# One load of decays for each head, behind the fetch of the triangular blocks, and a later rank for their work on ScalarE

## The chip, the cores and the metric

The kernel runs on one core of a Trainium2 chip. The metric is the device time of one execution in microseconds (us). The kernel before takes 782.92 us, the median of three runs (780.73, 782.92 and 783.98). A profile of one execution stands beside the runs; its own time is given with it below.

The engines are called PE (TensorE, matrix products), DVE (VectorE), ACT (ScalarE), POOL (GpSimd) and SP (SyncE, which here only issues transfers).

## What is computed

One layer of a decoder for 16 meta tokens and 512 tokens of width 1024, all in float32. Softmax attention and a chunked gated DeltaNet, 8 heads each, run side by side on the same normalised input; their gated outputs are merged, projected and normalised. The change lies in the DeltaNet branch, which for one head of 128 channels and chunks of tokens computes this (shortened from the reference):

```python
gc = jnp.cumsum(g, axis=-1)                      # log decays, summed within a chunk
diff = gc[..., :, None] - gc[..., None, :]
decay = jnp.where(incl, jnp.exp(diff), 0.0)      # incl: lower triangle with its diagonal
m = jnp.where(strict, einsum('bhnid,bhnjd->bhnij', kb, k) * decay, 0.0)
t_inv = triangular_solve(m + eye, eye, left_side=True, lower=True, unit_diagonal=True)
a_intra = einsum('bhnid,bhnjd->bhnij', q, k) * decay
q_dec = q * jnp.exp(gc)[..., None]
...
v_new = u_c - w_c @ state                        # chunk after chunk
o_c = qd_c @ state + a_c @ v_new
state = state * cd_c + kd_c.T @ v_new
```

So a head's summed log decays gc are used twice: in the matrix of decays (diff and decay) and in exp(gc), by which q is multiplied.

## The kernel before

**Planner.** The kernel is written as some dozens of generators (tasks). A task yields the name of an engine before it emits instructions on it, the name of an event that it waits for, or a tuple with the name of a buffer that it wants. A planner in the same file (class Plan, lines 82 to 192) runs all tasks against its own estimates of durations and so fixes the order of the instructions on every engine when the program is built. Among the tasks that want an engine it takes the one that can begin first, and among equals the one of lower rank; `spawn(gen, rank)` (line 107) sets the rank, and without one a task inherits the rank of the task that spawned it. On the chip each engine works its instructions off in that order; an instruction waits only for the data and the buffers that it needs, not for the planner's events. A load is reckoned by `transfer` (lines 127 to 131): it arrives 600 + 460 ns after its issue, plus its bytes at 360 bytes a nanosecond, plus 20 and 900 ns, later if other loads are under way.

**Tasks and ranks.** `dense` (rank 4) issues the big products of the projections, one block of 128 output channels after another: for each pair of heads k, v and q of the DeltaNet, then the attention's k, q, gate and v, and so on. A weight block is loaded (tile raw, four buffers), split by a cast on ACT (wh) and a subtraction on DVE (wl) into a high and a low part, and used in three passes; two blocks fit in split form. What follows a product (copies from the accumulator on ACT into xp or vT, the convolution and its tanh and gate: `conv_silu`, line 760) has rank 1. The pairs of heads of the DeltaNet (`delta_pair`, line 901) have rank 0, the attention heads rank 2.

**A pair of heads, gi.** `delta_pair` spawns for each of its two heads `decay`, `keys`, `values` and `products` (lines 1140 to 1144):

- `decay` (line 916) takes one of two buffers E, loads the head's row of summed log decays from a scratch tensor in DRAM (gcd) to all 128 partitions (256 KB), and makes the matrix of decays in place: four ACT instructions (Relu with a bias), one ACT exponential, one mask on POOL. For the second and later pairs it starts as soon as a buffer E is given back.
- `keys` and `values` transpose k and v on PE and evacuate them on ACT with scales (tiles ktd and vr).
- `products` (line 1007) multiplies k by k and k by q on PE. DVE evacuates the products with E into MT (the matrix m) and AT (a_intra). Four small DMAs per head write MT's diagonal 32 x 32 blocks to a scratch tensor (scrm), and E is given back (line 1069). Then the task takes the one buffer eg, loads the same row of gcd a second time, takes its exponential on ACT and multiplies q by it on DVE (lines 1070 to 1078).

When all blocks of a pair are written, they are fetched into the tile msub by two DMAs (`fetch`, line 1160), with two groups of blocks on separate partitions. Then DVE inverts them by forward substitution: 31 steps (line 1167) of two instructions each (tmps, then ts). The result goes through DRAM again (scrt, then td), and PE assembles the inverses of the chunks; `steps` (line 1319) runs the recurrence. Meanwhile the attention takes its turns with its scores (accumulator psc, ACT exponentials e, DVE maxima ast).

The buffers are counted in the dictionary SLOTS (line 68). `kernel` (line 1939) builds the program; it reserves 4096 bytes of scratch on each partition for DMAs whose descriptors software writes.

Of the kernel before, what the change touches and what calls it, by code (L numbers as in the profile page):

```python
# [10 lines left out]
F32 = mybir.dt.float32  # L11
F32R = mybir.dt.float32r
BF16 = mybir.dt.bfloat16
AF = mybir.ActivationFunctionType
ALU = mybir.AluOpType
# [3 lines left out]
P = 128  # L19
# [6 lines left out]
NC = SEQ // P  # L26
# [7 lines left out]
def dense_order():  # L34
# [11 lines left out]
    for p in range(KB // 2):  # L46
# [17 lines left out]
PE, DVE, ACT, POOL, SP = "PE", "DVE", "ACT", "POOL", "SP"  # L64

SLOTS = dict(raw=4, w=2, wo=4, W=4, sn=5, st=1, tf=1, psc=1, xp=2, y=2, kT=2, qT=2, ktd=2, vr=2, E=2, eg=1, AT=2, MT=2, sc=2, km=1,
             ts=1, msub=1, TT=1, aq=2, ak=1, vT=1, vs=1, e=4, pT=2, pm=2, ao=1, th=8)


# [10 lines left out]
class Plan:  # L82
# [24 lines left out]
    def spawn(self, gen, rank=None):  # L107
        time, src = self.here() if self.task else (0.0, SP)
        self.tasks.append(Task(gen, self.task.rank if rank is None else rank, time, src))

    def done(self, event):
        self.events[event] = self.here()
# [142 lines left out]
def hybrid_block(ctx: ExitStack, tc: tile.TileContext, x, meta, wblk, wbd, wout, pcol, prow, out):  # L255
    nc = tc.nc
    plan = Plan({**SLOTS, "wo": 0}, BANKS, ALL_BANKS)
    T, V, A, G, S = (Engine(plan, n, e) for n, e in
                     ((PE, nc.tensor), (DVE, nc.vector), (ACT, nc.scalar), (POOL, nc.gpsimd), (SP, nc.sync)))
    spawn, done = plan.spawn, plan.done  # L260
# [9 lines left out]
    def mk(pl, shape, dt, tag, bufs=None):  # L270
        uid[0] += 1
        kw = {} if bufs is None else {"bufs": bufs}
        return pl.tile(shape, dt, tag=tag, name=f"{tag}_{uid[0]}", **kw)
# [6 lines left out]
    dp = dctx.enter_context(tc.tile_pool(name="dp", bufs=1))  # L280
# [5 lines left out]
    def bank(kind):  # L286

        return mk(ps, [P, 2, 512], F32, kind, SLOTS[kind]) if kind == "psc" else banks_[plan.task.slot]

    def give(kind, at=None):  # L290
        plan.give(kind, names_.index(at.tensor.name) if kind in BANKS else 0)

    def slot(pl, shape, dt, tag):
        return mk(pl, shape, dt, tag, SLOTS[tag])

# [5 lines left out]
    def tick(event, n):  # L301
        ticks[event] = ticks.get(event, 0) + 1
        if ticks[event] == n:
            done(event)
# [3 lines left out]
    mt = mk(sp, [P, 2 * P], F32, "mt")  # L308
# [18 lines left out]
    msub = mk(dp, [P, 32, 32], F32, "msub")  # L327
# [59 lines left out]
    def split(n, raw):  # L387

        yield ("w" if n < len(ORDER) or n - len(ORDER) in (4, 5) else "wo",)
        if n < len(ORDER) or n - len(ORDER) in (4, 5):  # L390
            wh, wl = (mk(wp, [P, D], F32R, t, SLOTS["w"]) for t in ("wh", "wl"))
        else:
# [166 lines left out]
    def gates():  # L559
# [179 lines left out]
        late["ap"] = actx.enter_context(tc.tile_pool(name="ap", bufs=1, side="right"))  # L739
        late["pm"] = [mk(late["ap"], [P, 3, 32], F32R, f"pm{n}") for n in range(SLOTS["pm"])]  # L740
        late["vm"] = mk(late["ap"], [96, P], F32R, "vm")
# [11 lines left out]
    def chunk(c, o=NM):  # L753
        return slice(o + P * c, o + P * (c + 1))

    xps = [mk(dp, [P, L + 3], F32, f"xp{n}") for n in range(SLOTS["xp"])]
    for t in xps:
# [143 lines left out]
    def delta_pair(gi):  # L901
        hs = (2 * gi, 2 * gi + 1)
        E_, name = {}, lambda t: f"{t}/{gi}"
        kd, vr, at, mt = {}, {}, {}, {}
        scr = tc.dram_tile([33, 32, 32], F32, name=f"scrm{gi}")
        scrt = tc.dram_tile([33, 32, 32], F32, name=f"scrt{gi}")
        yield "ap"
# [1 line left out]
        sc = slot(dp, [P, 2, 4, 8], F32, "sc")  # L909
        yield ("km",)  # L910
        km, vm = slot(dp, [P, 32], F32, "km"), mk(dp, [P, 32], F32, "vm", SLOTS["km"])

        def gc_row(h):
            return gcd.rearrange("(c h) t -> h c t", h=8)[h].unsqueeze(0).broadcast_to([P, NC, P])

        def decay(i):

            h = hs[i]
            yield ("E",)
            e = slot(dp, [P, NC, P], F32, "E")  # L920
            yield SP
            S.dma_start(out=e, in_=gc_row(h))
            for c in range(NC):
                yield ACT
                A.activation(out=e[:, c, :], in_=e[:, c, :], func=AF.Relu, bias=gc[:, c, h:h + 1], scale=-1.0)
            yield ACT
            A.activation(out=e, in_=e, func=AF.Exp, scale=-1.0)
            yield POOL
            G.affine_select(out=e, in_=e, pattern=[[0, NC], [1, P]], base=0, channel_multiplier=-1,
                            compare_op=ALU.is_ge, fill=0.0)  # L930
            E_[i] = e
            done(f"E{h}")
# [74 lines left out]
        def products(i):  # L1007
            h = hs[i]
            yield f"dq{h}"
            yield f"dk{h}"  # L1010
            k = pair["k", h]
            q = pair["q", h]

            def norms():
                yield ("pdl",)
                yield PE
                pt = bank("pdl").rearrange("p (c d) -> p c d", d=P)
                for c in range(NC):
                    T.transpose(pt[:, c, :], q[:, chunk(c, 0)], ident)
                for c in range(NC):  # L1020
                    yield ACT
                    A.activation(out=mk(dp, [P, P], F32, "sqk", 1), in_=pt[:, c, :], func=AF.Square,
                                 accum_out=sc[:, i, c, qe_:qe_ + 1])
                give("pdl", pt)
                yield DVE
                V.tensor_scalar(out=sc[:, i, :, qe_], in0=sc[:, i, :, qe_], scalar1=128 * EPS, scalar2=128 * EPS * 4e-6,
                                op0=ALU.mult, op1=ALU.add)
                done(f"qe{h}")

            yield f"E{h}"  # L1030
            yield f"s{h}"
            yield ("MT",)
            mt[i] = slot(dp, [P, NC, P], F32, "MT")
            yield ("AT",)
            at[i] = slot(dp, [P, NC, P], F32, "AT")
            for c2 in range(0, NC, 2):
                yield ("pdl",)
                yield PE
                pg = bank("pdl").rearrange("p (c x) -> p c x", x=2 * P)
                for c in (c2, c2 + 1):  # L1040
                    T.matmul(pg[:, c - c2, 0:P], k[:, chunk(c)], k[:, chunk(c)], start=True, stop=True)
                    T.matmul(pg[:, c - c2, P:2 * P], k[:, chunk(c)], q[:, chunk(c, 0)], start=True, stop=True)

                def evac(c2=c2, pg=pg):
                    for c in (c2, c2 + 1):
                        yield DVE
                        V.scalar_tensor_tensor(out=mt[i][:, c, :], in0=pg[:, c - c2, 0:P], scalar=sc[:, i, c, s_:s_ + 1],
                                               in1=E_[i][:, c, :], op0=ALU.mult, op1=ALU.mult)
                    tick(f"m{h}", 2)
                    yield DVE  # L1050
                    V.tensor_tensor(out=at[i][:, c2:c2 + 2, :], in0=pg[:, :, P:2 * P], in1=E_[i][:, c2:c2 + 2, :], op=ALU.mult)
                    give("pdl", pg)
                    tick(f"a{h}", 2)

                spawn(evac())
            spawn(norms())
            yield f"m{h}"
            for b in range(4):

                def put(b=b):  # L1060
                    yield SP
                    S.dma_start(
                        out=scr[16 * i:16 * i + 16].rearrange("(c b) j i -> b j c i", b=4)[b],
                        in_=mt[i][32 * b:32 * b + 32, :, 32 * b:32 * b + 32])
                    tick(name("scr"), 9)

                spawn(put())
            yield f"a{h}"
            give("E")
            yield ("eg",)  # L1070
            yield SP
            eg = slot(dp, [P, NC, P], F32, "eg")
            S.dma_start(out=eg, in_=gc_row(h))
            yield ACT
            A.activation(out=eg, in_=eg, func=AF.Exp)
            yield DVE
            V.tensor_tensor(out=q, in0=q, in1=eg.rearrange("p c t -> p (c t)"), op=ALU.mult)
            give("eg")
            done(f"qd{h}")

# [57 lines left out]
            tick(name("scr"), 9)  # L1138

        for i in range(2):  # L1140
            spawn(decay(i))
            spawn(keys(i))
            spawn(values(i))
            spawn(products(i))
# [22 lines left out]
        for j in range(31):  # L1167
            n, w = 31 - j, min(j + 1, 16)
# [3 lines left out]
                            in1=ts_[0:97, j, 0:w].unsqueeze(1).broadcast_to([97, n, w]), op=ALU.mult)  # L1172
# [723 lines left out]
    def deltas():  # L1896
        for gi in range(H // 2):
            spawn(delta_pair(gi))
            yield "ap"
# [54 lines left out]
```

## Time and profile before

| | before |
|---|---|
| median of 3 runs | 782.92 us |
| profiled execution, whole time | 781.9 us |
| its span, first to last instruction | 780.1 us |
| granted TensorE clock, mean | 0.996 |
| PE busy | 752.8 us (96%) |
| DVE busy | 566.0 us (73%) |
| ACT busy | 477.2 us (61%) |
| POOL busy | 68.3 us (9%) |
| issues of E from gcd, and of eg from gcd | 8 and 8, 256 KB each |

In rows of the timeline the columns are the start in us, the busy time in us, the engine, the line, the operation, output and inputs, their shapes, the count; a bracket gives the engine's idle time just before and who ended it. All operations have line 220, a helper that records each of them, so rows are told apart by their tiles: `MT<-bank,sc,E` writes MT from an accumulator bank, sc and E. A q behind an engine's name (SPq) marks its queue: such a row is the issue of a transfer, not its landing. In rows of stretches the columns are the stretch, its length, the busy time and count of PE, of its weight loads, of DVE, ACT and POOL, then the granted clock of PE as a share of full speed, the DMA engines' share and GB/s. Heads are counted from 0, pairs too: pair 1 is heads 2 and 3.

### The profile page before, as it was taken

The page shows a single profiled execution, that of the slowest core. Times are in us where ns is not written, and L with a number is a line of the kernel's source. Part 1 is how long each engine was busy: PE and PEld are TensorE (multiplying, and loading weights), DVE is VectorE, ACT ScalarE, POOL GpSimd, SP SyncE. Part 2 cuts the span into 40 slices and gives each one's busy share as a digit, 9 for nine tenths or more (in the row PEclk, how much of TensorE's full clock was granted, in tenths as well). Part 3 has the DMA queues.
Part 4 walks back from the last instruction along what each step waited for, and adds up shares of the span by engine and source line. Part 5 has one row for each costly group of instructions (what it writes and reads, how often), then busy time and mean ns, then how long its engine had stood idle before and what let it go on. Part 6 is the DMA issues. An engine that isn't in the chain of part 4 may idle for free.

```text
span 780.1 us, 14404 instructions
## 1 busy us (share of the span) xinstructions
PE 752.8 (96%) x5479; PEld 689.1 (88%) x5479; DVE 566.0 (73%) x1287; ACT 477.2 (61%) x1272; POOL 68.3 (9%) x98
## 2 busy tenths in 40 slices
PE   5999999999999999999999999999999999999996
PEld 4999788999987899998789998888988998899786
DVE  6767698477769767767956766995678868789553
ACT  5375747688564768765486975467776436444432
POOL 3120002021000202100020220000000000000001
PEclk9999999999999999999999999999999999999999
DMA  8132533111333301234220124222023322332702
GB/s 307 32 116 70 120 102 72 52 55 56 112 99 89 88 29 55 68 111 115 82 68 29 56 80 124 88 82 69 28 66 100 134 58 105 108 109 85 266 0 109
DMA packets 45470, 70.10 MB, mean 90 GB/s; under 512 B 20273, under 2 KB 28881, under 8 KB 45401
## 3 DMA queue, kind: packets, MB, share of 16 engines
q1 hardware_dynamic: 45400, 69.18, 28.8%
q8 instruction: 43, 0.70, 0.4%
q14 instruction: 27, 0.21, 0.1%
HBM read 65.98 MB, written 3.19 MB: 89 GB/s over the span
## 4 chain that ended last, share of the span: by engine, by line
PE 70%; DVE 11%; DMA 9%; ACT 5%; issue 2%; SPq 2%; POOL 1%; POOLq 0%; ACTq 0%; DVEq 0%
PE bank L220 66%; PE psc L220 3%; DMA msub<-scrm 3%; DVE wl L220 2%; DMA eg<-gcd 2%; DVE tmps L220 2%; SPq L220 2%; DVE ts L220 2%; DMA scrt<-ts 2%; ACT wh L220 1%; DMA td<-scrt 1%; DMA xt<-in_x_dram 1%; DVE aq L220 1%; ACT E L220 1%; DMA E<-gcd 1%
## 5 line engine op out<-in xcount | busy, mean ns | idle before, releaser
L220 PE MATMUL bank<-hnH,wh 128*128 128x512 f32 (+3 forms) x944 | 317.4, 338 | 1.0 <-ACT hnH L220 0.8
L220 PE MATMUL bank<-hnH,wl 128*128 128x512 f32 (+3 forms) x944 | 302.3, 322 | 2.3 <-DVE wl L220 2.3
L220 PE MATMUL bank<-hnL,wh 128*128 128x512 f32 (+3 forms) x944 | 301.9, 322 | 0.0
L220 PEld LDWEIGHTS bank<-hnH,wl 128*128 128x128 f32 x944 | 177.6, 189 | 17.2 <-DVE wl L220 3.2
L220 PEld LDWEIGHTS bank<-hnH,wh 128*128 128x128 f32 x944 | 178.0, 189 | 14.6 <-ACT hnH L220 1.0
L220 PEld LDWEIGHTS bank<-hnL,wh 128*128 128x128 f32 x944 | 178.1, 190 | 10.2
L220 DVE TENSOR_TENSOR wl<-raw,wh 128x1024 fp32r<-128x1024 f32 x82 | 100.3, 1223 | 51.9 <-ACT wh L220 51.0
L220 ACT CAST wh<-raw 128x1024 fp32r<-128x1024 f32 x82 | 86.0, 1048 | 39.5 <-PE bank L220 24.1
L220 DVE SCALAR_TENSOR_TENSOR y<-xp,pc,y 128x528 f32<-128x528 f32 (+1 forms) x72 | 54.2, 756 | 1.4 <-ACT y L220 0.4
L220 ACT ACTIVATE e<-psc,ast 128x144 f32<-128x144 f32 (+3 forms) x64 | 34.4, 539 | 23.1 <-DVE ast L220 18.6
L220 DVE TENSOR_TENSOR tmps<-msub,ts 97x240 f32<-97x240 f32 (+27 forms) x124 | 39.1, 316 | 7.6 <-DMA msub<-scrm 5.7
L220 DVE TENSOR_TENSOR ts<-ts,tmps 97x240 f32<-97x240 f32 (+27 forms) x124 | 39.7, 320 | 2.2
L220 PE MATMUL bank<-btH,Wh 128*128 128x256 f32 x128 | 35.9, 280 | 0.0
L220 PE MATMUL bank<-btL,Wh 128*128 128x256 f32 x128 | 35.7, 279 | 0.0
L220 PE MATMUL bank<-btH,Wl 128*128 128x256 f32 x128 | 35.7, 279 | 0.0
L220 PE MATMUL psc<-ak,aq 128*128 128x264 f32 (+3 forms) x160 | 29.4, 305 | 4.1 <-ACT e L220 4.1
L220 ACT CAST Wh<-raw 128x1024 fp32r<-128x1024 f32 (+1 forms) x24 | 21.7, 906 | 17.7 <-PE bank L220 11.6
L220 PEld LDWEIGHTS psc<-ak,aq 128*128 128x128 f32 x160 | 23.7, 189 | 6.7 <-ACT e L220 5.4
L220 DVE TENSOR_TENSOR Wl<-raw,Wh 128x1024 fp32r<-128x1024 f32 (+1 forms) x24 | 24.9, 1044 | 6.4 <-ACT Wh L220 6.3
L220 DVE TENSOR_REDUCE ast<-psc 128x1 f32<-128x528 f32 (+3 forms) x40 | 28.5, 714 | 0.2
L220 ACT ACTIVATE sqk<-bank 128x128 f32<-128x128 f32 x64 | 17.8, 278 | 13.5 <-PE bank L220 12.5
L220 ACT COPY sn<-bank 128x256 f32<-128x256 f32 x24 | 9.0, 374 | 26.5 <-PE bank L220 26.4
(335 smaller groups left out, 1508.8 us busy)
## 6 DMA issues: line engine op xcount, KB each, us to landing
raw<-in_wblk_dram SPq DMA_DIRECT2D x96, 512.0 KB, 3.5
raw<-in_wout_dram SPq DMA_DIRECT2D x8, 512.0 KB, 5.2
xt<-in_x_dram SPq DMA_DIRECT2D x4, 512.0 KB, 3.5
E<-gcd SPq DMA_DIRECT2D x8, 256.0 KB, 6.0
eg<-gcd SPq DMA_DIRECT2D x8, 256.0 KB, 6.0
xr<-in_x_dram SPq DMA_DIRECT2D x8, 256.0 KB
out_dram<-xr SPq DMA_DIRECT2D x8, 256.0 KB, 2.1
msub<-scrm SPq DMA_DIRECT2D x8, 132.0 KB
```

Source lines behind the costliest of these rows:

```text
L220: return real(*args, **kw)
```

## The change

- `decay` has a second output: after the load of E it takes a buffer eg, writes the exponential of E into it on ACT, and goes on with E as before. `products` uses this eg and no longer loads or computes it. There are two buffers eg in place of one, and they are held from `decay` to the multiplication of q.
- For all pairs but the first, `decay` waits in the planner for the event that the previous pair's triangular blocks have been fetched (msub).
- `decay` is spawned with rank 2 in place of the inherited 0. This covers its load, its ACT instructions and its mask.
- The scratch for DMAs by software is 1024 bytes in place of 4096.

```diff
-... E=2, eg=1, ...
+... E=2, eg=2, ...
...
-        kd, vr, at, mt = {}, {}, {}, {}
+        kd, vr, at, mt, eg = {}, {}, {}, {}, {}
...
         def decay(i):

             h = hs[i]
+            if gi:
+                yield f"msub/{gi - 1}"
             yield ("E",)
             e = slot(dp, [P, NC, P], F32, "E")
             yield SP
             S.dma_start(out=e, in_=gc_row(h))
+            yield ("eg",)
+            eg[i] = slot(dp, [P, NC, P], F32, "eg")
+            yield ACT
+            A.activation(out=eg[i], in_=e, func=AF.Exp)
             for c in range(NC):
                 yield ACT
                 A.activation(out=e[:, c, :], in_=e[:, c, :], func=AF.Relu, bias=gc[:, c, h:h + 1], scale=-1.0)
...
             yield f"a{h}"
             give("E")
-            yield ("eg",)
-            yield SP
-            eg = slot(dp, [P, NC, P], F32, "eg")
-            S.dma_start(out=eg, in_=gc_row(h))
-            yield ACT
-            A.activation(out=eg, in_=eg, func=AF.Exp)
             yield DVE
-            V.tensor_tensor(out=q, in0=q, in1=eg.rearrange("p c t -> p (c t)"), op=ALU.mult)
+            V.tensor_tensor(out=q, in0=q, in1=eg[i].rearrange("p c t -> p (c t)"), op=ALU.mult)
             give("eg")
...
         for i in range(2):
-            spawn(decay(i))
+            spawn(decay(i), 2)
             spawn(keys(i))
...
-    nc = _bacc.Bacc("TRN2", target_bir_lowering=False, num_devices=1, dynamic_dma_scratch_size=4096)
+    nc = _bacc.Bacc("TRN2", target_bir_lowering=False, num_devices=1, dynamic_dma_scratch_size=1024)
```

More of the change, by code (lines that the diff above doesn't have):

```diff
@@ L64 @@
 PE, DVE, ACT, POOL, SP = "PE", "DVE", "ACT", "POOL", "SP"
-SLOTS = dict(raw=4, w=2, wo=4, W=4, sn=5, st=1, tf=1, psc=1, xp=2, y=2, kT=2, qT=2, ktd=2, vr=2, E=2, eg=1, AT=2, MT=2, sc=2, km=1,
+SLOTS = dict(raw=4, w=2, wo=4, W=4, sn=5, st=1, tf=1, psc=1, xp=2, y=2, kT=2, qT=2, ktd=2, vr=2, E=2, eg=2, AT=2, MT=2, sc=2, km=1,
              ts=1, msub=1, TT=1, aq=2, ak=1, vT=1, vs=1, e=4, pT=2, pm=2, ao=1, th=8)
```

## The prediction

> **What bounds the kernel now.** I read the page first, then the waits of PE, PE's timeline at each of those waits, and the busy time in stretches of 10 us.
>
> ```profile
> span 780.1 us, 14404 instructions
> ...
> PE 752.8 (96%) x5479; PEld 689.1 (88%) x5479; DVE 566.0 (73%) x1287; ACT 477.2 (61%) x1272; POOL 68.3 (9%) x98
> ```
>
> PE (TensorE) is busy for 752.8 of 780.1 us, so 27.3 us is all that any reordering can win. No matmul is added or removed here, so the question is only which of those idle stretches go and which new ones come.
>
> ```profile
> PE bank L220 <- ACT sq L220: 7.7, 1, 7.7
> PE psc L220 <- ACT e L220: 4.1, 3, 1.9
> PE bank L220 <- DVE wl L220: 2.3, 2, 1.4
> PE bank L220 <- DVE y L220: 1.8, 2, 1.3
> ```
>
> The columns are total us, times, longest. The first row is the start of the kernel and not touched. The other three lie in the loop over head pairs; in time they are these (the bracket is PE's idle time before the instruction, and who ended it):
>
> ```profile
> 58.85 0.33 PE L220 MATMUL bank<-ident,y 128*128 128x128 f32 x1 [1.32 <-DVE y L220]
> ...
> 88.14 0.39 PE L220 MATMUL bank<-hnH,wh 128*128 128x272 f32 x1 [0.25 <-ACT wh L220]
> ...
> 90.05 0.39 PE L220 MATMUL bank<-hnH,wl 128*128 128x272 f32 x1 [1.39 <-DVE wl L220]
> ...
> 228.62 0.50 PE L220 MATMUL bank<-hnH,wl 128*128 128x512 f32 x1 [0.88 <-DVE wl L220]
> ...
> 242.47 0.39 PE L220 MATMUL psc<-ak,aq 128*128 128x272 f32 x1 [1.90 <-ACT e L220]
> ...
> 374.91 0.39 PE L220 MATMUL psc<-ak,aq 128*128 128x272 f32 x1 [1.86 <-ACT e L220]
> ...
> 505.81 0.39 PE L220 MATMUL psc<-ak,aq 128*128 128x272 f32 x1 [0.36 <-ACT e L220]
> ```
>
> There is one more loss, which no wait shows:
>
> ```profile
> 90.00:100.00 10.00, 9.95 (x59) 9.37 (x60) 9.39 (x23) 6.53 (x12) 0.64 (x1) 0.83 0.36 107
> ...
> 770.00:780.00 10.00, 4.08 (x35) 3.88 (x33) 3.39 (x10) 2.46 (x6) 1.59 (x2) 0.87 0.28 106
> ```
>
> The third number from the right is the granted clock. It is 0.83 in the 10 us behind the idle of 1.39 us at 90.05, which is worth 10 x 0.17 = 1.7 us of PE's work. The last row is the tail, where PE is idle for 5.9 us. So the middle holds 27.3 - 7.7 - 5.9 = 13.7 us of idle time, and 1.7 us of slow clock: 15.4 us is the bound of any gain.
>
> **The change part by part.** Part one: the second load of each row of decays (eg) goes, and eg comes from the tile E before E is overwritten. Part two: from the second pair on, a head's load stands behind the fetch of the previous pair's triangular blocks (msub). The rows of pair 1 (heads 2 and 3) and of pair 3 show what stands ahead of that fetch on SP's queue now:
>
> ```profile
> 215.65 0.38 SPq L220 DMA_DIRECT2D eg<-gcd  x1
> 216.14 0.44 SPq L220 DMA_DIRECT2D E<-gcd  x1
> 216.76 0.70 SPq L220 DMA_DIRECT2D msub<-scrm  x2
> ...
> 480.71 0.38 SPq L220 DMA_DIRECT2D eg<-gcd  x1
> ...
> 481.86 0.69 SPq L220 DMA_DIRECT2D msub<-scrm  x2
> ```
>
> ```profile
> E<-gcd SPq DMA_DIRECT2D x8, 256.0 KB, 6.0
> eg<-gcd SPq DMA_DIRECT2D x8, 256.0 KB, 6.0
> ...
> td<-scrt SPq DMA_DIRECT2D x4, 128.0 KB, 2.4
> ```
>
> ```profile
> 87.95 0.19 DVE L220 TENSOR_TENSOR tmps<-msub,ts 97x31 f32<-97x31 f32 x1 [2.65 <-DMA msub<-scrm]
> ...
> 223.81 0.19 DVE L220 TENSOR_TENSOR tmps<-msub,ts 97x31 f32<-97x31 f32 x1 [1.28 <-DMA msub<-scrm]
> ...
> 356.26 0.19 DVE L220 TENSOR_TENSOR tmps<-msub,ts 97x31 f32<-97x31 f32 x1 [1.74 <-DMA msub<-scrm]
> ...
> 486.93 0.18 DVE L220 TENSOR_TENSOR tmps<-msub,ts 97x31 f32<-97x31 f32 x1
> ```
>
> A load of decays takes 6.0 us to land. In pair 1 two of them are issued just ahead of the fetch, and the substitution on DVE (tmps) starts at 223.81, 7.05 us after the fetch's issue. In pair 3 only one stands there, and it starts at 486.93, 5.07 us after. With none ahead, the nearest row is td, 128 KB from a scratch tensor of the same kind in 2.4 us. So the blocks can be there 2.7 us (pair 3) to 4.6 us (pair 1) earlier, and DVE's three idle waits of 2.65, 1.28 and 1.74 us go.
>
> What is that worth to PE? The pairs hold the answer already. Between the first tmps and the matmul into psc that waits lie 242.47 - 223.81 = 18.66 us in pair 1, 374.91 - 356.26 = 18.65 us in pair 2 and 505.81 - 486.93 = 18.88 us in pair 3: DVE works that stretch through without a gap, so the matmul waits for the start of the substitution. Pair 3, which starts its substitution sooner after the fetch (by 2 us), waits 0.36 us there, against 1.90 and 1.86. I take that for pairs 1 and 2: 1.54 + 1.50 = **3.0 us won** (0 if DVE's order in the new plan puts as much ahead; 4.1 if all three go).
>
> Pair 0's idle of 0.25 + 1.39 us comes from the eg load itself:
>
> ```profile
> 86.52 0.63 ACT L220 ACTIVATE eg<-eg 128x512 f32<-128x512 f32 x1 [1.96 <-DMA eg<-gcd]
> 87.06 1.03 ACT L220 CAST wh<-raw 128x1024 fp32r<-128x1024 f32 x1
> ```
>
> ```profile
> ACT eg L220 <- DMA eg<-gcd: 11.1, 8, 2.3
> ...
> DVE qT L220 <- ACT eg L220: 11.2, 7, 3.9
> ```
>
> ACT (ScalarE) stands 1.96 us at eg with the cast of the next weights (wh) queued behind it; DVE's wl waits for that cast and PE for wl. With eg made from E long before, both waits of these rows go, 11.1 us on ACT and 11.2 us on DVE; only this one of the eight reached PE. **Won: 1.64 us, and the 1.7 us of half clock that follow it, 3.3 us** (bounds: 1.6 without the clock, 3.3 with it). The Trainium skill, "TensorE: Matmul & The Clock Gate", Part 1 and its summary of rules, has the clock drop after a whole idle window of about 3.4 us and asks only that gaps stay under some 3 us. By that rule no gap above could have cost clock, and this term would be 1.6 us. The row of 90 to 100 us speaks against it; the idle of 1.90 us at 242.47, with a clock of 1.00 in its stretch below, agrees with it.
>
> Part three, the rank. In pair 0 the decays' ACT work stands ahead of copies that PE needs:
>
> ```profile
> 52.63 2.46 ACT L220 ACTIVATE E<-E,gc 128x128 f32<-128x128 f32 x8
> 54.98 1.16 ACT L220 ACTIVATE E<-E 128x512 f32<-128x512 f32 x2
> ...
> 57.43 0.62 ACT L220 ACTIVATE xp<-y 128x528 f32<-128x528 f32 x1
> ```
>
> ```profile
> 58.09 0.71 DVE L220 SCALAR_TENSOR_TENSOR y<-xp,y 128x528 f32<-128x528 f32 x1 [2.24 <-ACT xp L220]
> ...
> 69.91 0.35 DVE L220 SCALAR_TENSOR_TENSOR MT<-bank,sc,E 128x128 f32<-128x128 f32 x1
> ```
>
> E takes ACT from 52.63 to 56.14, 3.5 us, the tanh into xp comes at 57.43, and PE's idle of 1.32 us at 58.85 waits for what DVE makes of it. E itself is read first at 69.91. At rank 2 it moves behind the copies, into some of the 13.8 us to spare, and with it go two exponentials (eg) of 0.63 us that are new in this place. **Won: 1.3 us** (0 if the freed place on ACT is taken by another task of rank 0; should the two exponentials find no gap, 1.3 us is lost instead).
>
> The idle of 0.88 us at 228.62 I leave as it is: the next pair's loads come behind the fetch, so E's work on ACT lands near there as before.
>
> **What it adds.** Only the planner waits for the event of the fetch; on the chip the load stands behind the fetch on SP's in-order queue. E's buffers are given back before the last blocks are written, so nothing is waited for there, and the weight loads (raw) behind it lose its issue of 0.4 to 0.5 us and its place in the transfer, which four raw buffers hide; without that cover it is 6.0 us a load. But the planner reckons a load of 256 KB at 600 + 460 + 728 + 20 + 900 ns = 2.7 us (lines 127 to 131) and it takes 6.0, so ACT is sent to E up to 3.3 us too soon, in order, with casts of weights behind it. That is what happened at 86.52 with eg. There will be six such loads (two heads, pairs 1 to 3). One of the eight waits on eg cost PE 3.3 us: 6/8 x 3.3 = **2.5 us lost** (bounds: 0, and 3 x 3.3 = 9.9 us if each pair's wait reaches PE whole).
>
> ```profile
> q1 hardware_dynamic: 45400, 69.18, 28.8%
> ```
>
> That eight of sixteen such loads go wins nothing more in itself: the one queue that carries data fills 28.8% of its engines' time. The second eg buffer and the smaller scratch are room in memory, which I cost at nothing.
>
> **The sum.** -3.0 - 3.3 - 1.3 + 2.5 = -5.1 us. The profiled execution took 781.9 us (span 780.1), so its like would take 776.8; the median of the runs, 782.9, is 1.0 above it, and I forecast 782.9 - 5.1 = 777.8 us.
>
> By the rule of the Trainium skill, "TensorE: Matmul & The Clock Gate", on the clock, the sum would be -3.0 - 1.6 - 1.3 + 6/8 x 1.64 = -4.7, an estimate 0.4 us from mine.
>
> **The rivals.**
>
> ```profile
> 230.00:240.00 10.00, 10.00 (x50) 8.13 (x49) 9.46 (x23) 2.65 (x5) 0.00 (x0) 1.00 0.28 95
> 240.00:250.00 10.00, 8.10 (x62) 7.63 (x61) 9.77 (x29) 4.88 (x14) 0.00 (x0) 1.00 0.35 107
> ```
>
> (1) *Given back on DVE, no change.* The plan is made anew, and DVE is full in the substitution (third column: 9.46 and 9.77 of 10 us). If the substitution starts sooner but DVE's other work is packed in ahead of the psc chain, the 3.0 us stay; with the rest, -3.3 - 1.3 + 2.5 = -2.1: 780.8 us. For it: the planner believed in 2.7 us all along, so its plan has no room that the chip lacked. Against it: pair 3. (2) *Slower: ACT stands at E.* In each of pairs 1 to 3 ACT waits the full 3.3 us at the first load, with wh behind it, and PE stops that long and loses 1.7 us of clock: 3 x 5.0 = 15.0 lost against 7.6 won, +7.4: 790.3 us. It decides from about 2 us of wait on: the longest wait for eg that PE did not feel was 2.3 us, the one that it felt 1.96. Against it: rank 2 puts E behind whatever else is ready, and ACT is busy for only 2.65 and 4.88 of 10 us there. (3) *The order does not change*, or nothing hangs on it: SP was free anyway, and the fetch is late for its own sake. Then ACT's waits and the clock stay too, and only the rank is left, 781.6 us. Against it: 7.05 us with two loads ahead, 5.07 with one.
>
> **How the numbers follow.** 0.5% is 3.9 us, about what a measurement of this kernel can tell from no change (the three runs lie between 780.73 and 783.98). Chances: the forecast 0.56, rival 1 0.24, rival 2 0.12, rival 3 0.08. Faster by over 0.5% means under 779.0, only 1.2 us above the forecast: most of its chance and a little of rival 1's, 0.52. Same: 0.36, the rest of both and rival 3. Slower: 0.12, rival 2. The range begins where all goes well: -4.1 - 3.3 - 1.3 and nothing lost, 774.2, rounded to 774; above, it takes in rivals 1 and 3 and the weaker half of rival 2, and the spread of the runs, to 784; the rest of rival 2 is left out.
>
> **What would show it.** Right: eight loads of E and none of eg; on SP, E after msub in pairs 0 to 2; the first tmps without idle time and some 2.5 to 4 us after the fetch's issue; no PE wait at psc over 0.5 us; no wait for y near 58 us; granted clock 1.00 from 20 to 770 us. Wrong: ACT rows of eg with 2 us and more of waiting for E's load and PE rows waiting for wl right behind them; a PE idle total in the middle that is still 13 us, with other names.

## The result: slower by a quarter of a per cent

The changed kernel takes 784.16 us, the median of 15 runs (781.88 to 786.78), beside 782.46 us (780.73 to 783.98, 15 runs) for the kernel before, measured with it. The ratio is 1.0024 with a 95% interval of 1.0012 to 1.0035. The forecast was 777.8 us, faster; the result lies just above the range and on the other side of no change.

The page of the changed kernel, its profiled execution:

```profile
span 782.5 us, 14429 instructions
...
PE 753.3 (96%) x5479; PEld 689.6 (88%) x5479; DVE 570.3 (73%) x1287; ACT 473.9 (61%) x1272; POOL 68.0 (9%) x98
...
E<-gcd SPq DMA_DIRECT2D x8, 256.0 KB
```

There are eight loads of E and none of eg, as the change says. PE is idle for 782.5 - 753.3 = 29.2 us, against 27.3 before. So idle time went and other idle time came. The waits of all engines and of PE show both (us in total, times, longest):

```profile
ACT eg L220 <- DMA E<-gcd: 18.2, 6, 6.1
...
DVE aq L220 <- ACT aq L220: 7.6, 3, 5.1
...
DVE tmps L220 <- DMA msub<-scrm: 0.2, 1, 0.2
```

```profile
PE psc L220 <- ACT e L220: 4.5, 3, 2.2
PE bank L220 <- ACT sqm L220: 2.0, 1, 2.0
PE bank L220 <- DVE ms L220: 2.0, 1, 2.0
...
PE bank L220 <- ACT wh L220: 1.3, 1, 1.3
```

DVE's waits for the blocks are gone but for 0.2 us (5.7 us before), and so are its waits for eg (11.2 us). But ACT now stands 18.2 us at eg, for the load of E, where it stood 11.1 us for the load of eg. In time, PE's idle places are these:

```profile
55.89 0.22 PE L220 MATMUL bank<-ones,sqm 128*32 128x1 f32 x2 [1.97 <-ACT sqm L220]
...
60.17 0.33 PE L220 MATMUL bank<-ident,y 128*128 128x128 f32 x1 [1.95 <-DVE ms L220]
...
98.24 0.50 PE L220 MATMUL bank<-hnH,wh 128*128 128x512 f32 x1 [1.28 <-ACT wh L220]
...
99.50 0.50 PE L220 MATMUL bank<-hnH,wl 128*128 128x512 f32 x1 [0.53 <-DVE wl L220]
...
114.23 0.39 PE L220 MATMUL psc<-ak,aq 128*128 128x272 f32 x1 [2.17 <-ACT e L220]
...
243.81 0.39 PE L220 MATMUL psc<-ak,aq 128*128 128x272 f32 x1 [1.38 <-ACT e L220]
...
375.77 0.39 PE L220 MATMUL psc<-ak,aq 128*128 128x272 f32 x1 [0.94 <-ACT e L220]
```

The loss lies ahead of 115 us: 1.97 + 1.95 + 1.28 + 0.53 + 2.17 = 7.9 us, where the kernel before lost 1.32 + 0.46 + 0.25 + 1.39 = 3.4 us (0.46 us of it near 65 us). From there on the changed kernel is the better one: at psc PE waits 1.38 + 0.94 us in place of 1.90 + 1.86 + 0.36 us. Here is the origin on ACT, with the load's issue on SP:

```profile
46.41 0.98 SPq L220 DMA_DIRECT2D E<-gcd  x2
```

```profile
45.76 0.74 ACT L220 ACTIVATE y<-xp,pc 128x528 f32<-128x528 f32 x1
51.25 0.63 ACT L220 ACTIVATE eg<-E 128x512 f32<-128x512 f32 x1 [4.75 <-DMA E<-gcd]
52.29 0.63 ACT L220 ACTIVATE eg<-E 128x512 f32<-128x512 f32 x1 [0.41 <-DMA E<-gcd]
52.83 0.26 ACT L220 ACTIVATE sqk<-bank 128x128 f32<-128x128 f32 x1
...
94.18 0.63 ACT L220 ACTIVATE eg<-E 128x512 f32<-128x512 f32 x1 [6.12 <-DMA E<-gcd]
94.84 0.59 ACT L220 ACTIVATE aq<-bank 64x512 fp32r<-64x512 f32 x1
```

The load is issued at 46.41 and ACT goes to its exponential right behind its work of 45.76. It stands there for 4.75 us, with squares, copies and casts queued behind it, and PE runs dry twice. In pair 1 it stands for 6.12 us, with the copy aq out of an accumulator behind it, for which DVE waits 5.1 us in the middle of pair 0's substitution, and with the cast wh behind that, for which PE waits 1.28 us at 98.24. The two other long waits are 4.18 us in pair 2, at 228.01, and 1.94 + 0.82 us in pair 3, near 358.

ACT went too soon, and by more than the 3.3 us of the forecast. The code has the reason. In the changed `decay` the wait for the buffer eg stands between the load and the exponential. A task that asks for a buffer after a load is set back to the load's issue (`Plan.wait`: `if task.issued is not None and isinstance(task.want, tuple): task.time = task.issued`). Its use, as I read it, is that a chain of loads need not wait for one another's landing. Here it forgets that E has not landed, and it takes the exponential to be ready when the load is issued.

### The profile page after: what moved, and what is told of

It reads as the page before. It is cut to its first block, busy times and chain, and to the rows that moved or that the text cites. A ratio compares the mean times of both kernels' runs of the same rounds, so it can differ in the third digit from the quotient of the medians.

```text
span 782.5 us, 14429 instructions
## 1 busy us (share of the span) xinstructions
PE 753.3 (96%) x5479; PEld 689.6 (88%) x5479; DVE 570.3 (73%) x1287; ACT 473.9 (61%) x1272; POOL 68.0 (9%) x98
## 4 chain that ended last, share of the span: by engine, by line
PE 76%; DVE 9%; ACT 5%; DMA 5%; issue 2%; POOL 2%; SPq 1%; POOLq 0%; ACTq 0%; DVEq 0%
PE bank L220 73%; PE psc L220 3%; DVE wl L220 3%; DMA E<-gcd 2%; DVE tmps L220 2%; DVE ts L220 2%; DMA scrt<-ts 1%; ACT wh L220 1%; POOL ts L220 1%; DMA xt<-in_x_dram 1%; ACT sqk L220 1%; ACT ak L220 1%; SPq L220 1%; ACT TT L220 0%; DVE ast L220 0%
## 5 line engine op out<-in xcount | busy, mean ns | idle before, releaser
L220 ACT ACTIVATE sqk<-bank 128x128 f32<-128x128 f32 x64 | 17.7, 276 | 14.6 <-PE bank L220 13.9
```

The costliest lines, as they stand in the source:

```text
L220: return real(*args, **kw)
```

## The experiments

My theory after this comparison: the planner loses the landing time, and ACT's waits on that account are the loss (*slot*). The rivals: the new plan as such, with DVE full in the substitution (*reshuffle*); and the planner's short reckoning of a load, 2.7 us in place of 6.0, which the forecast had named. Ratios are to the kernel before, measured beside each run, with their 95% intervals.

**slot_first.** The changed kernel with eg taken before the load:

```diff
             e = slot(dp, [P, NC, P], F32, "E")
+            yield ("eg",)
+            eg[i] = slot(dp, [P, NC, P], F32, "eg")
             yield SP
             S.dma_start(out=e, in_=gc_row(h))
-            yield ("eg",)
-            eg[i] = slot(dp, [P, NC, P], F32, "eg")
```

> The changed kernel with one pair of lines exchanged: decay takes its buffer eg before the load of E and not between the load and the exponential. Theory (slot): in the changed kernel the planner forgets when the load lands. A task that waits for a buffer after a load is set back to the time of the load's issue (Plan.wait), so ACT is sent to the exponential of E at once, and stood idle there for 18.2 us in 6 waits, up to 6.1 us each. Then this kernel's ACT waits for E should fall below 10 us in all (the 2.7 us that the planner reckons are then kept), PE's idle of 1.97 and 1.95 us near 54 and 58 us, the half clock behind them and the 2.17 us at 112 us should go, and the time should fall by 4 to 6 us, to 778 to 780. Rival (reshuffle): the loss is the new plan as such, DVE being full, and the waits of ACT are covered; then the time stays within 1.5 us of the changed kernel, 782.5 to 785.5.

770.1 us, ratio 0.9849 (0.9825 to 0.9874): 14 us below the changed kernel, where I expected 4 to 6. Its waits on ACT and the stretches around pair 0:

```profile
ACT eg L220 <- DMA E<-gcd: 1.5, 3, 0.8
```

```profile
50.00:60.00 10.00, 10.00 (x88) 9.82 (x87) 7.28 (x21) 9.97 (x33) 2.75 (x4) 1.00 0.35 93
60.00:70.00 10.00, 10.00 (x86) 9.99 (x86) 7.84 (x14) 8.03 (x21) 2.26 (x3) 1.00 0.35 107
```

The changed kernel in the same stretches:

```profile
50.00:60.00 10.00, 6.25 (x53) 5.80 (x52) 2.99 (x11) 8.18 (x33) 2.04 (x2) 1.00 0.19 46
60.00:70.00 10.00, 9.83 (x70) 9.81 (x71) 7.38 (x16) 9.06 (x25) 1.66 (x5) 0.83 0.27 95
```

The first number behind the length is PE's busy time. It rises from 6.25 to 10.00 us at 50 to 60, and the half clock behind it (0.83) is gone: 3.75 + 0.17 + 1.7 = 5.6 us from this place alone (a half clock of the same size came near 130 us instead, see the last section). The rest of the 14 us lies later, and I did not add it up place by place.

**slot_first_6us.** As slot_first, and after the load `plan.arrival += 3300`, which puts the landing that the planner reckons with 3300 ns later.

> As slot_first, and the planner is told that this load lands 3.3 us later, 6.0 us after its issue, as the trace has it. If the forecast's cost of loads (ACT sent to E up to 3.3 us too soon) is real beside the slot, ACT's waits for E fall to 2 us or less in all and the time is another 1 to 3 us below slot_first. If only the slot matters, the two are within 1 us of each other.

767.75 us, ratio 0.9823 (0.98 to 0.9847), with once_rank_6us below the fastest kernel here; ACT's waits for E are no longer listed. On the same chip the medians differ by 2.4 us and no run of the one reaches a run of the other (767.58 to 768.74 against 769.35 to 770.91), though the intervals of the ratios overlap. So the true landing time is worth something beside the slot, some 2 us. Its page:

```profile
span 765.9 us, 14407 instructions
...
PE 748.1 (98%) x5479; PEld 688.6 (90%) x5479; DVE 568.0 (74%) x1287; ACT 477.4 (62%) x1272; POOL 70.1 (9%) x98
```

**before_6us.** The kernel before with `plan.arrival += 3300` after its loads of E and of eg, nothing else.

> The kernel before, with the planner told that its loads of E and eg land 6.0 us after their issue and not 2.7. If the planner's too short loads are what costs in the kernel before (ACT's 11.1 us of waits for eg, PE's 1.64 us and the half clock near 90 us), the time falls by 2 to 4 us, to 779 to 781, with no other edit. If loading once is needed for that, it stays within 1 us of 782.5.

772.65 us, ratio 0.9882 (0.9858 to 0.9905). The true landing time wins 9 us in the kernel before, with all sixteen loads in place, where I expected 2 to 4. So most of what the best kernels here win lay in a plan made on a wrong estimate, and not in the second load. DVE waits 8.4 us for the fetch in this kernel (5.7 us in the kernel before), and still PE's waits at psc come to 0.6 us (4.1 us).

**rank_only.** The kernel before with `spawn(decay(i), 2)`.

> The kernel before with the rank of decay alone changed to 2. The forecast's third part: PE's idle of 1.32 us at 58.85 goes, and with it 1 to 2 us of the time, 780.5 to 781.5. Rival (reshuffle): the stall moves, and the time is anywhere within 2 us of 782.5.

782.89 us, ratio 1.0008 (0.9992 to 1.0023): no change, as the rival had it and not the forecast. The wait near 58 us went, and ACT's waits for eg stayed (11.7 us); PE's waits at psc rose from 4.1 to 7.0 us:

```profile
PE psc L220 <- ACT e L220: 7.0, 3, 2.6
```

**once_rank, slot_first_rank0, once_only.** slot_first without the wait for the fetch, slot_first without the rank, and slot_first without either:

```diff
-            if gi:
-                yield f"msub/{gi - 1}"
```

```diff
-            spawn(decay(i), 2)
+            spawn(decay(i))
```

> slot_first without the wait for the fetch: one load a head, eg taken before it, rank 2, but the next pair's loads may stand ahead of the fetch of the triangular blocks again. By the forecast's step (a load ahead of the fetch delays the substitution, and the substitution ends PE's wait at psc) msub lands some 2 us later than in slot_first in pairs 0 to 2, PE waits at psc again, and the time is 2 to 4 us above slot_first's 770.1. If the fetch was not what mattered, the two are within 1 us.

> slot_first with decay at rank 0 as in the kernel before. By the forecast's step for the rank, PE waits 1.3 us near 58 us again and the time is 771 to 772.5. After rank_only, which changed nothing (782.9 against 782.1), I rather expect within 1.5 us of 770.1, of either sign.

> Loading once and nothing else: eg taken before the load, no wait for the fetch, rank 0. If the second load and the waits for it are most of the gain of slot_first, 771 to 774; if the order behind the fetch is, 778 to 782.

Ratios 0.9858 (0.9838 to 0.9877), 0.9864 (0.9846 to 0.9882) and 0.9895 (0.9877 to 0.9912). The medians are 771.91, 772.94 and 775.03 us. Loading once alone holds 8 of the 12 us of slot_first; its time is just above the 771 to 774 us expected. Taken out of slot_first one at a time, the wait for the fetch and the rank make about 1 us each, within the intervals; only both together (0.9895 against 0.9849) stand clear of them. Added to once_only one at a time, on one chip, each wins more: 3.1 us the rank (once_rank) and 2.1 us the wait for the fetch (slot_first_rank0), and no run of once_only (773.71 to 776.16) reaches theirs (771.53 to 773.11). So the two do not add up either. For once_rank the forecast's step for the fetch had 2 to 4 us above slot_first; by the ratios it is 0.7 us.

**gate_only.** The kernel before with the two lines of the wait for the fetch.

> The kernel before with the wait for the fetch alone: the next pair's load of E comes behind the fetch, the loads of eg stay ahead of it. One load ahead of the fetch in place of two, as in pair 3 of the kernel before: msub some 2 us sooner in pairs 1 and 2, PE's waits of 1.90 and 1.86 us at psc down to 0.4, 3 us won, 779 us. The rival (ACT sent to E and eg too soon as before decides) gives 781 to 783.

779.76 us, ratio 0.9966 (0.9952 to 0.998): 2.7 us won, near the forecast's price of 3.0 us for the fetch. The kept trace does not show the way to it. It is of a run of 783.22 us, where nine of the twelve runs lie between 779.02 and 780.30. ACT's waits for eg come to 13.9 us in it, and these are pairs 1 and 2:

```profile
223.14 0.69 DVE L220 TENSOR_TENSOR qT<-qT,eg 128x512 f32<-128x512 f32 x1 [2.60 <-ACT eg L220]
223.75 0.18 DVE L220 TENSOR_TENSOR tmps<-msub,ts 97x31 f32<-97x31 f32 x1
...
243.18 0.59 PE L220 MATMUL psc<-ak,aq 128*128 128x272 f32 x1 [2.83 <-ACT e L220]
...
356.67 0.18 DVE L220 TENSOR_TENSOR tmps<-msub,ts 97x31 f32<-97x31 f32 x1
...
375.88 0.39 PE L220 MATMUL psc<-ak,aq 128*128 128x272 f32 x1 [0.72 <-ACT e L220]
```

The fetch is issued at 218.59 and 351.10, so the substitution starts 5.16 and 5.57 us after it, in place of 7.05 and 7.13 us, and no longer waits for it; now it stands behind a wait for eg (2.60 us in pair 1). But PE waits at psc for 2.83 and 0.72 us, 3.55 us together where the kernel before has 3.76. So the blocks are there sooner after the fetch's issue, as expected, and PE's waits hardly fell with that in this run. Where the 2.7 us of the median come from is not shown.

**slot_first_0us.** slot_first with `plan.arrival = plan.end` after the load: the planner takes it to have landed at once. The instructions stand in the order of the changed kernel on every engine.

> slot_first, with the planner told that the load has landed when it is issued. If what costs in the changed kernel is that its planner loses the landing time (and not that the buffer eg is taken late), this kernel is as slow as the changed one, 783 to 785.5, with ACT waiting some 18 us for E. If the place of the buffer matters, it stays near slot_first's 770.

783.83 us, ratio 1.0013 (0.9997 to 1.0029), and on ACT

```profile
ACT eg L220 <- DMA E<-gcd: 17.1, 6, 5.8
```

So the landing time that the planner reckons with makes the whole difference of 13 to 14 us to slot_first, and not the place of the buffer. Reshuffle in the form stated, ACT's waits being covered, fell with slot_first. What stays true of it is that every run here has a new order on all engines: the difference is the price of the landing time with the plan that it leads to, and not of ACT's waits alone.

**slot_pair0 and slot_later.** eg before the load only in the first pair (`if not gi`), or only in the later ones (`if gi`).

> The changed kernel with eg taken before the load in the first pair alone. The forecast looked for the cost of loads planned too soon in pairs 1 to 3 and left pair 0 out. By the comparison of PE's products in the two traces, slot_first is 5.7 us ahead of the changed kernel by 60 us, before any other pair's load: 784.2 - 5.7 = 778.5 us expected (777 to 780). If pairs 1 to 3 hold the loss, 783 to 785.

> The changed kernel with eg taken before the load in pairs 1 to 3 alone, so that pair 0's ACT stands at E for 4.8 us as in the changed kernel. The rest of the loss goes: 784.2 - 14.1 + 5.7 = 775.8 us (774 to 778). If the two halves do not add up, the losses hide one another and it is nearer to 784 or 770.

773.22 us, ratio 0.9876 (0.9853 to 0.9899), and 775.03 us, ratio 0.9891 (0.9868 to 0.9914). Against the changed kernel (ratio 1.0024) the first half alone wins 11.6 us, where I expected 5.7, and the second 10.4 us; both together, slot_first, win 13.7 us (0.0175 x 782.5). So the parts hide one another. A place where that shows is pair 1 in slot_pair0. Its own loads are as wrongly planned as in the changed kernel, yet ACT stands there for 1.48 us and not 6.12:

```profile
84.61 1.38 ACT L220 ACTIVATE eg<-E 128x512 f32<-128x512 f32 x2 [1.48 <-DMA E<-gcd]
```

Why it stands so much shorter in the plan made anew was not taken apart. Nor does a wait of ACT tell its price by its length. In pair 3 of slot_pair0 ACT stands 4.16 us at eg, about as long as in pair 2 of the changed kernel, and the kernel is still 11.6 us faster.

**once_rank_6us.** slot_first_6us without the wait for the fetch.

> slot_first_6us without the wait for the fetch: what the place behind the fetch is worth once the planner knows the load's true time. In the pair slot_first and once_rank it was about 1 us (ratios 0.9849 and 0.9858). With loads ahead of it the fetch lands some 2 us later: 769 to 771 if that reaches PE, 767 to 768.5 if not.

768.77 us, ratio 0.9816 (0.9793 to 0.984), the same as slot_first_6us within the intervals. DVE waits 2.8 us for the fetch again, and PE has no wait at psc. Beside before_6us (0.9882) this prices loading once, with the later rank, when the planner knows the landing time: 5 us more.

## Why the prediction was wrong, step by step

- **The bound** (15.4 us to win in the middle) held: the best kernels here won 1.8%, some 14 us. What it was added up from did not quite hold. The span of slot_first_6us is 780.1 - 765.9 = 14.2 us shorter than that of the kernel before, with 9.5 us less idle time of PE and 4.7 us less busy time. The slow clock is 1.7 us of the latter; the other 3.0 us are in the same 5479 matmuls, whose busy time the forecast took as fixed, and were not taken apart.
- **The fetch** (3.0 us won): right in its first half. In the changed kernel the substitution starts 4.7, 3.3, 4.4 and 3.0 us after the fetch's issue, where it took 7.05 us in pair 1 and 5.07 us in pair 3, and DVE waits for it 0.2 us in all. The second half was that the matmul into psc follows the start of the substitution at a fixed distance (18.65 to 18.88 us). It is 24.83, 20.58 and 19.06 us in pairs 0 to 2 of the changed kernel; in pair 0, DVE's wait of 5.1 us for ACT lies within it. PE's waits at psc in pairs 1 to 3 fell from 1.90, 1.86 and 0.36 us to 1.38, 0.94 and none, 1.8 us in place of 3.0; a new one of 2.17 us came in pair 0. Alone, the wait for the fetch won 2.7 us, near the price, by a way that its trace does not show. Once the planner knows the load's time, it wins nothing that can be measured.
- **The second load** (3.3 us won): the waits named are gone, near 90 us, with the half clock that followed. In the changed kernel waits of the same kind (1.28 us for wh and 0.53 us for wl) stand near 98 us behind ACT's wait for E, and the half clock near 62 us, so nothing of this was won there. Loading once without the rank and the wait for the fetch (once_only) won 8.2 us, and the kernel before with both loads won 9 us by the landing time alone: the step named the second load, and the runs point to the time at which the planner sent ACT to it.
- **The rank** (1.3 us won): failed. The wait at 58.85 us went in rank_only and its price came back elsewhere; in the changed kernel the place lost 3.9 us. By the code, rank orders only tasks that can begin at one time; eg was taken to be ready at the load's issue, so rank 2 did not put it behind the copies of a moment later.
- **What it adds** is the step that failed: "ACT is sent to E up to 3.3 us too soon", "six such loads (two heads, pairs 1 to 3)", "2.5 us lost". The mechanism stood there, and rival 2 was built on it. But pair 0 was left out, because its load was not moved, though eg's exponential was moved up to it; and the planner did not think 2.7 us, it thought none, because of the buffer wait between load and exponential, which I had in the diff and did not follow through `Plan.wait`. The waits measured were 4.75, 6.12 and 4.18 us in pairs 0 to 2, over the 3.3 us that the step allowed, and 1.94 us in pair 3. The forecast's sign of being wrong, ACT rows of eg with 2 us and more of waiting for E's load, is there. Against the kernel with that one order mended the step costs 13.7 us, not 2.5, and it took all that the other steps won (11.8 us by the ratio of slot_first) and 1.9 us more. It lies above the step's upper bound of 9.9 us too. What the step did describe, a landing believed in at 2.7 us and not at 6.0, is the 2.4 us between slot_first and slot_first_6us, near its 2.5; that the sizes agree is in part luck, since pair 0 is in the one and not in the other.

## What to carry to other kernels

Where an order of instructions is fixed ahead of time on estimates, an instruction that is placed before its data lands holds up everything behind it on its engine (ACT for up to 6.12 us here); so when an edit moves a load's reader, look for what the planner takes as its ready time, also at the first repetition, which the edit seems not to touch. In such a kernel, compare the planner's durations with the trace before changing the program: here one true landing time was worth 9 us without any other edit. Parts of such a change do not add up; price them by running each with and without the others.

## What the runs showed of the hardware

The granted clock fell behind short idle times: 0.83 over a stretch of 10 us, as half speed for 3.4 us would give. In single microseconds of the kernel before it was 0.62, 0.50, 0.50 and 0.67, which loses 1.71 us in all:

```profile
91.00:92.00 1.00, 1.00 (x8) 1.00 (x6) 0.94 (x2) 0.98 (x2) 0.00 (x0) 0.62 0.85 176
92.00:93.00 1.00, 1.00 (x6) 1.00 (x6) 0.93 (x3) 0.98 (x2) 0.46 (x1) 0.50 0.86 348
93.00:94.00 1.00, 1.00 (x6) 1.00 (x6) 0.93 (x3) 0.98 (x2) 0.17 (x1) 0.50 0.08 16
94.00:95.00 1.00, 1.00 (x8) 1.00 (x7) 0.97 (x3) 0.97 (x3) 0.00 (x0) 0.67 0.00 0
```

In the changed kernel the dip (0.83 in the stretch of 60 to 70 us) follows two waits of 1.97 and 1.95 us. In slot_first there is one in the stretch of 130 to 140 us, where PE's only listed wait nearby is 0.49 us:

```profile
120.00:130.00 10.00, 9.51 (x87) 8.20 (x86) 6.25 (x13) 6.40 (x19) 4.30 (x6) 1.00 0.37 78
130.00:140.00 10.00, 10.00 (x112) 9.42 (x112) 4.28 (x9) 8.54 (x18) 0.00 (x0) 0.83 0.18 52
```

The idle of 2.17 us at 114.23 us in the changed kernel had no dip behind it, nor had the 2.64 us at 243.43 us in rank_only. The Trainium skill, "TensorE: Matmul & The Clock Gate", Part 1, ties the drop to one idle window of some 3.4 us, and tells further on of a kernel in which frequent short idle times brought it too. The dip's length agrees with that window; its onset here does not need an idle time that long. Neither does the length of the idle time decide it, as the figures above show, and what does was not tried.
